# Down-projection of two token blocks by seven half-size products, with its weight and activation sums on GpSimd

## The chip, the cores and the metric

The kernel runs on one core of a Trainium2 chip. The metric is the time of one execution on the device, in microseconds. It is to be as short as possible.

## What is computed

One layer of a streaming encoder works on 2,048 prompt tokens and 128 sample tokens (8 requests of 16) of width 1,024: 17 tiles of 128 tokens. A combined projection feeds chunked attention and an mLSTM; their outputs are normalised, projected and added to the residual (the "mixers" below). Then comes a gated feed-forward part, which the change is about. In the reference:

```python
def conv_ffn(h, buf, w_up, w_conv, b_conv, w_down):
    S = h.shape[1]
    u = h @ w_up                                  # 1024 -> 2 x 2816
    ext = jnp.concatenate([buf.astype(u.dtype), u], axis=1)
    y = b_conv
    for j in range(CONV_W):                       # causal, width 3
        y = y + ext[:, j:j + S] * w_conv[j]
    gate, up = jnp.split(y, 2, axis=-1)
    out = (jax.nn.gelu(gate, approximate=True) * up) @ w_down   # 2816 -> 1024
    return out, ext[:, S:]
```

Everything is float32.

## The kernel before

**Precision.** TensorE gets its float32 operands split into a rounded high part (a cast on ScalarE, L1265) and the rest (a subtraction on VectorE, L1266). `mm3` (L93) makes one product out of three matmuls: high x high, high x low, low x high.

**Order of the work.** Python loops write out the whole program; a list scheduler then orders each engine's instructions by a simulated time line. In the mixers, projections in 14 weight groups for each half of the tokens are interleaved with steps of attention, mLSTM and normalisation. Row-wide loads there use the tile `xr`, of which there are two buffers.

**The feed-forward part** takes the tiles in three blocks: tiles 0 to 5, 6 to 11, and 12 to 15 with the sample tile. For each block:

- *Up stage* (the loop at L1478). 22 slices f of 128 features, each for gate and up. A slice is already computed as seven half-size products in Winograd's form (`product`, L1411): 7 x 4 x 3 = 84 matmuls of 384 columns. The sums of the up weights are made by VectorE in block 0 and kept in DRAM (`load_quads`, L1270 and L1282); later blocks read them. VectorE joins the products out of PSUM (L1419, L1491, L1493, L1508), does two of the convolution's three taps (L1439, L1440) and multiplies gate by up (L1514) into a tile `g` of 128 x 768. GpSimd copies the convolution's two history columns (`conv`, L1428). The tile `g` is stored to DRAM (`gd`, L1519).
- *Down stage* (the loop at L1525). For each half of the 1,024 output columns, the 22 slices of `g` are read back (`fetch`, L1454), split (`split_g`, L1465) and multiplied by weights (`load_down`, L1311) for 6 tiles at a time, in 6 PSUM accumulators. `evacuate` (L1334) copies an accumulator out on VectorE and sums its squares on ScalarE; the halves go to DRAM. Meanwhile the next block's input is normalised, transposed and summed (`h2_units`, L1057), and the previous block's outputs are finished (`later`, L1369: one operation on VectorE, an addition on GpSimd, L1377, and a store from GpSimd's queue).

**Buffers.** Loads of 512 columns use 11 "quads" (L1048), loads and results of up to 1,024 columns 4 "rows" (L1051). Nearly all loads and stores are issued in order by SyncE (SP).

Of the kernel before, what the change touches and what calls it, by code (L numbers as in the profile page):

```python
# [10 lines left out]
F32 = mybir.dt.float32  # L11
# [6 lines left out]
P = 128  # L18
# [19 lines left out]
FBLOCKS = [[0, 1, 2, 3, 4, 5], [6, 7, 8, 9, 10, 11], [12, 13, 14, 15, SAMPLE]]  # L38
HALF = [384, 384, 320]
PAIRS = [[(((b[j], 0), (b[j + 3], 0)), j * P, P, f"{b[j]}") for j in range(3)] for b in FBLOCKS[:2]]  # L40
PAIRS += [[(((12, 0), (15, 0)), 0, P, "12"), (((13, 0), (SAMPLE, 0)), P, P, "13"), (((14, 0), (14, 64)), 2 * P, 64, "14")]]


@with_exitstack
def hymba_step(ctx: ExitStack, tc: tile.TileContext, I: dict, O: dict):
# [17 lines left out]
    def dt_(shape, name):  # L63
        return dram.tile(shape, F32, tag=name, name=name)
# [48 lines left out]
    gd = [[dt_([P, 768], f"gd{b}_{f}") for f in range(NF)] for b in range(len(FBLOCKS))]  # L113
    wsd = [dt_([P, 2048], f"wsd{f}") for f in range(NF)]
    lated = [dt_([P, 4, 384], f"lated{i}") for i in range(4)]
    x2d = [dt_([P, D], f"x2d{t}") for t in range(17)]
# [928 lines left out]
        pipes[:] = [Pipe(h2_units(0, lead=6)), Pipe(iter([]))]  # L1045

    def quad(name):
        return ffn.p3.tile([P, 512], F32, tag="q", name=name, bufs=11)  # L1048

    def row(name):  # L1050
        return ffn.p3.tile([P, D], F32, tag="yq", name=name, bufs=4)  # L1051

    def new_B(i, b):
        pool = ffn.p3 if i < EARLY_B else ffn.p4
# [90 lines left out]
    def late_B():  # L1145

        for i in (P5, P2, P4, P3):
# [3 lines left out]
            nc.scalar.copy(hi, lo.bitcast(F32))  # L1151
            nc.vector.tensor_tensor(lo, lo.bitcast(F32), hi, op=ALU.subtract)

    GROUPS = ["va0", "qk0", "qk1", "va1", "qk2", "qk3", "qb0", "vo0", "qb1", "vo1", "qb2", "vo2", "qb3", "vo3"]
    SRC = {g: i for i, g in enumerate(["va0", "qk0", "qk1", "va1", "qk2", "qk3",
                                       "qb0", "vo0", "qb1", "vo1", "qb2", "vo2", "qb3", "vo3"])}
# [36 lines left out]
    chunks = []  # L1193
    norms = norm_steps(0)
    next(norms)
    pend = load_group(0)
    for _ in pend[2]:
        pass
# [2 lines left out]
    for n_, (half, gi) in enumerate(seq):  # L1201
        wh, wl, _ = pend
        split = iter([])
        if n_ + 1 < len(seq):
            pend = load_group(seq[n_ + 1][1])
            split = pend[2]
        g = GROUPS[gi]
        i = int(g[2])
        nm = f"{g}_{half}"
        if g[:2] == "va":  # L1210
            it = group_rows(wh, wl, half, chunks, vd[i], nm, 264 if gi == 0 else 256,
                            [O["v_prompt"][i], O["v_sample"][i].unsqueeze(1)])
        elif g[:2] == "qk":
            it = group_T(wh, wl, half, chunks, [qTd[i], kTd[i]], [-(DA ** -0.5), None], nm,
                         [None, [O["k_prompt"][i], O["k_sample"][i]]])
        elif g[:2] == "qb":
            it = group_T(wh, wl, half, chunks, [[t_[:, c, :] for t_ in qkbd[i]] for c in range(2)],
                         [None, DH ** -0.5], nm)
        else:
            it = group_rows(wh, wl, half, chunks, vobd[i], nm)  # L1220
        if half == 0 and gi == 13:
            chunks = []
            norms = norm_steps(1)
        if n_ == len(seq) - 1:
            out = project([0, 1, 2, 3, 4, 5, 6, 7, SAMPLE, 8, 9, 10, 11, 12, 13, 14, 15])
            split = w_out_steps()
            next(split)
            next(out)
        for u, (pe, dve) in enumerate(it):
            ahead = []  # L1230
            if n_ < len(seq) - 1 or u >= 6:
                ahead.append(next(split, (0.0, 0.0)))
            if n_ == len(seq) - 1 and u == 12:
                ahead.append(next(out))
            if (half == 0 and gi == 13 and u >= 6 and u % 2 == 0) or (gi == 0 and u % 2 == 0):
                ahead.append(next(norms, (0.0, 0.0)))
            pump(pe + sum(a[0] for a in ahead), dve + sum(a[1] for a in ahead))
        for _ in split:
            pass
        if gi == 0:  # L1240
            if half == 0:
                nc.sync.dma_start(bgate, I["b_gate"].broadcast_to([P, 8]))
                nc.sync.dma_start(gatt, I["g_att"])
                heads.append(build_bias)
                mems.append(lambda: prep(prep_sample()))
            mems.append(lambda half=half: prep(prep_prompt(half)))
        if g[:2] == "qk":
            attention(i, half)
            if half == 0 and i == 3:
                heads.insert(len(heads) % 4, lambda: attention_sample(0, EARLY))  # L1250
            if half == 1 and i == 0:
                heads.insert(len(heads) % 4, lambda: attention_sample(EARLY, DB))
        if g[:2] == "vo":
            mems.append(lambda i=i, half=half: mlstm(i, half))
            if half == 0:
                mems.append(lambda i=i: mlstm_sample(i))
# [37 lines left out]
            out.append(r)  # L1294
        return out

    def load_up(b, f, g, quads=None):
        n = 2 * f + g
# [12 lines left out]
    def load_down(dh, c):  # L1311
        n = 4 if c < 5 else 2
        src = I["w_down"][dh, 2 * c:2 * c + n // 2].rearrange("a p n -> p a n")
        h_ = wpool.tile([P, 2112], F32R, tag="wh", name=f"wdh{dh}_{c}", bufs=2)
        l_ = wpool.tile([P, 2112], F32R, tag="wl", name=f"wdl{dh}_{c}", bufs=2)
        for a in range(n // 2):
            for e in range(2):
                cc = slice(a * 1024 + e * 512, a * 1024 + e * 512 + 512)
                raw = quad(f"wdr{dh}_{c}_{a}_{e}")
                nc.sync.dma_start(raw, src[:, a, e * 512:e * 512 + 512])  # L1320
                split(h_[:, cc], l_[:, cc], raw)
        return h_, l_

    pair = [None]

# [77 lines left out]
    for b, tiles in enumerate(FBLOCKS):  # L1403
# [41 lines left out]
        def ahead_of(i):  # L1445
            if i < 2 * NF:
                pend.append(load_up(b, i // 2, i % 2))
            elif i == 2 * NF:
                pend.append(load_down(0, 0))

        g, parts = {}, {}
        n2 = nt * P // 2
# [1 line left out]
        def fetch(dh, k, early=False):  # L1454
            if dh > 1 or k >= NF:
                return
            if early:
                g[dh, k] = [quad(f"gr{b}_{dh}_{k}_{i}")[:, :n2] for i in range(2)]
                for i, r in enumerate(g[dh, k]):
                    nc.sync.dma_start(r, gd[b][k][:, i * n2:(i + 1) * n2])  # L1460
            else:
                g[dh, k] = row(f"gr{b}_{dh}_{k}")
                nc.sync.dma_start(g[dh, k][:, :2 * n2], gd[b][k][:, :2 * n2])
# [11 lines left out]
        def w3_tile(name):  # L1475
            return p4.tile([P, 1056], F32R, tag="w3", name=name, bufs=4)

        for f in range(NF):  # L1478
            w = pend.pop(0)
            ahead_of(2 * f + 2)  # L1480
            if f == NF - 2:
                fetch(0, 0, True)
                fetch(0, 1, True)
# [11 lines left out]
            uu = u_tile(f"uu{nm}")  # L1495
            second(uu, x3, c)
            w = pend.pop(0)
            ahead_of(2 * f + 3)
            if f == NF - 1:
                split_g(0, 0, w3_tile)  # L1500
                split_g(0, 1, w3_tile)
                for k in range(2, 5):
                    fetch(0, k, True)
# [15 lines left out]
            nc.sync.dma_start(gd[b][f][:, :nt * P], gt[:, :nt * P])  # L1519
# [4 lines left out]
        res = {}  # L1524
        for dh in range(2):  # L1525
            mms = [ps_mm(f"dnm{b}_{dh}_{i}") for i in range(2)]
            bigs = [ps_big(f"dn{b}_{dh}_{i}") for i in range(2)]
# [77 lines left out]
def lay_inputs(inp):  # L1605
# [15 lines left out]
    w_up = np.stack([w_up[:, :, 0, 0], w_up[:, :, 0, 1], w_up[:, :, 1, 1], w_up[:, :, 1, 0]], 2)  # L1621
    wc = np.concatenate([inp["w_conv"][0], inp["b_conv"]], 0)
    out = {
        "x_prompt": inp["x_prompt"][0],
# [11 lines left out]
        "w_down": inp["w_down"][0].reshape(NF // 2, 2, P, 2, 512).transpose(3, 0, 2, 1, 4).reshape(2, NF // 2, P, 1024),  # L1636
# [58 lines left out]
```

## Time and profile before

| | |
|---|---|
| runs, median (lowest to highest) | 2794.89 us (2793.72 to 2796.46) |
| profiled execution, first to last instruction | 2784.7 us |
| mixers up to the first up-projection | about 1313 us |
| up stage, block 0 / 1 | 328 / 318 us |
| down stage, block 0 / 1 | 195 / 194 us |
| up and down stage of the last block, to the end | 435 us |
| granted TensorE clock, mean | 0.998 |

The page gives the profiled execution's span alone; the median of the runs is 10.2 us longer, which is what lies outside the first and last instruction. In the profile PE is TensorE's matmuls, PEld its weight loads (which overlap the matmuls), DVE VectorE, ACT ScalarE, POOL GpSimd, SP SyncE. A line such as L1266 is that line of the kernel before. Stages follow each other; their ends are those of the first and last matmul of their kind.

### The profile page before, as it was taken

The numbers are of one execution on the slowest core, as the hardware profiler recorded it, in microseconds if no ns is written. First come the engines' busy times: TensorE is split into PE (matmuls) and PEld (weight loads), VectorE is DVE, ScalarE is ACT, GpSimd is POOL, SyncE is SP. The second block draws the span as 40 slices with busy tenths as digits, with TensorE's granted clock in tenths as the row PEclk, the third lists the DMA queues.
The fourth block names the chain that finished last, engine by engine and source line by source line (L and its number), as shares of the span: only waits on it lengthen the run. The fifth ranks groups of instructions, "written<-read, shape, count | busy, mean of one in ns | idle before, by whom it ended". The sixth has DMA issues, their size and how long they took to land.

```text
span 2784.7 us, 47088 instructions
## 1 busy us (share of the span) xinstructions
PE 2723.8 (98%) x16587; PEld 2548.3 (92%) x16587; DVE 1876.3 (67%) x3447; ACT 1409.1 (51%) x2836; POOL 437.4 (16%) x895
## 2 busy tenths in 40 slices
PE   8999999999999999999999999999999999999998
PEld 7899999998899998888999988899999878999887
DVE  5344455656556668666999986457877864888855
ACT  4355555644356666544454555345455543555543
POOL 1000010212000003244111110011111310222220
PEclk9999999999999999999999999999999999999999
DMA  5544355557555555356655455644544774555585
GB/s 185 155 119 136 103 174 162 164 157 217 162 173 148 144 179 171 107 176 227 187 172 167 167 176 174 219 142 153 160 152 141 276 263 152 172 179 180 192 309 190
DMA packets 311883, 486.05 MB, mean 175 GB/s; under 512 B 55426, under 2 KB 150622, under 8 KB 311518
## 3 DMA queue, kind: packets, MB, share of 16 engines
q1 hardware_dynamic: 271134, 442.92, 50.1%
q10 hardware_dynamic: 38592, 33.83, 3.6%
q0 software_dynamic: 1920, 6.29, 0.6%
q8 instruction: 130, 2.13, 0.3%
q14 instruction: 107, 0.88, 0.1%
HBM read 359.36 MB, written 126.70 MB: 175 GB/s over the span
## 4 chain that ended last, share of the span: by engine, by line
PE 55%; DVE 2%; DMA 1%; issue 1%; ACT 1%; POOL 1%; SPq 0%; DVEq 0%; POOLq 0%; ACTq 0%
PE uec L95 6%; PE uec L96 6%; PE uec L97 6%; PE dn L97 4%; PE dn L96 4%; PE dn L95 4%; PE ua L97 3%; PE ua L95 3%; PE ua L96 3%; PE dnm L97 2%; PE dnm L95 2%; PE dnm L96 2%; PE wo L97 2%; PE wo L95 2%; PE wo L96 2%; PE ub L96 1%
## 5 line engine op out<-in xcount | busy, mean ns | idle before, releaser
L95 PE MATMUL uec<-B,wuh 128*128 128x384 f32 (+1 forms) x720 | 234.9, 328 | 2.2 <-DVE uu L1419 1.1
L96 PE MATMUL uec<-B,wuh 128*128 128x384 f32 (+1 forms) x720 | 235.1, 327 | 0.0
L97 PE MATMUL uec<-B,wul 128*128 128x384 f32 (+1 forms) x720 | 233.9, 327 | 0.0
L1266 DVE TENSOR_TENSOR gl<-gr,gh 128x768 fp32r<-128x768 f32 (+3 forms) x141 | 120.4, 863 | 145.8 <-ACT gh L1265 144.5
L1265 ACT CAST gh<-gr 128x768 fp32r<-128x768 f32 (+3 forms) x141 | 102.0, 735 | 200.1 <-PE dn L96 183.2
L1265 ACT CAST wuh<-wu 128x512 fp32r<-128x512 f32 x255 | 141.7, 617 | 112.1 <-PE uec L96 103.2
L95 PE MATMUL dn<-wdh,gh 128*128 128x512 f32 x466 | 182.4, 391 | 2.3 <-DVE ug L1419 2.3
L96 PE MATMUL dn<-wdl,gh 128*128 128x512 f32 x466 | 183.4, 394 | 0.0
L97 PE MATMUL dn<-wdh,gl 128*128 128x512 f32 x466 | 167.9, 396 | 0.0
L1266 DVE TENSOR_TENSOR wul<-wu,wuh 128x512 fp32r<-128x512 f32 x255 | 164.6, 683 | 2.8 <-DMA x2d<-mx 2.8
L393 DVE CUSTOM_DVE_ANT_0 tmp<-s,nb 128x640 f32<-128x640 f32 (+4 forms) x128 | 94.4, 737 | 96.6 <-PE s L383 94.8
L95 PE MATMUL vo<-wi_h,hT 128*128 128x256 f32 x544 | 155.1, 285 | 0.6 <-DVE mt L199 0.6
L97 PE MATMUL vo<-wi_h,hT 128*128 128x256 f32 x544 | 155.6, 286 | 0.0
L96 PE MATMUL vo<-wi_l,hT 128*128 128x256 f32 x544 | 154.8, 285 | 0.0
L95 PEld LDWEIGHTS uec<-B,wuh 128*128 128x128 f32 x720 | 135.0, 188 | 4.2 <-DVE uu L1419 1.6
L95 PE MATMUL qk<-hT,wi_h 128*128 128x384 f32 (+1 forms) x384 | 128.7, 335 | 7.4 <-ACT qk_st L224 6.6
L96 PEld LDWEIGHTS uec<-B,wuh 128*128 128x128 f32 x720 | 135.2, 188 | 0.2
L97 PEld LDWEIGHTS uec<-B,wul 128*128 128x128 f32 x720 | 135.1, 188 | 0.0
L406 DVE TENSOR_TENSOR ptl<-pt,pth 128x640 fp32r<-128x640 f32 (+4 forms) x128 | 93.6, 737 | 57.1 <-ACT pth L405 56.0
L394 ACT ACTIVATE tmp<-tmp,mn 128x640 f32<-128x640 f32 (+4 forms) x128 | 97.6, 762 | 64.6 <-DVE mn L393 61.9
L96 PE MATMUL qb<-hT,wi_h 128*128 128x384 f32 (+1 forms) x384 | 127.8, 333 | 0.0
L96 PE MATMUL qk<-hT,wi_h 128*128 128x384 f32 (+1 forms) x384 | 127.6, 332 | 0.0
(412 smaller groups left out, 8873.0 us busy)
## 6 DMA issues: line engine op xcount, KB each, us to landing
wu<-in_w_up SPq DMA_DIRECT2D x220, 256.0 KB, 4.1
wu<-wsd SPq DMA_DIRECT2D x176, 256.0 KB, 4.2
wdr<-in_w_down SPq DMA_DIRECT2D x132, 256.0 KB, 5.6
gr<-gd SPq DMA_DIRECT2D x78, 384.0 KB, 3.6
wi_raw<-in_w_in SPq DMA_DIRECT2D x52, 512.0 KB, 4.0
wsd<-ws SPq DMA_DIRECT2D x88, 256.0 KB, 2.8
gd<-g SPq DMA_DIRECT2D x44, 384.0 KB, 3.5
kraw<-kTd SPq DMA_DIRECT2D x112, 128.0 KB, 3.2
```

Of the source, the lines that this page charges most:

```text
L95: nc.tensor.matmul(out, ah, bh, start=start, stop=False, skip_group_check=onto)
L96: nc.tensor.matmul(out, ah, bl, start=False, stop=False, skip_group_check=onto)
L97: nc.tensor.matmul(out, al, bh, start=False, stop=stop, skip_group_check=onto)
L393: nc.vector.tensor_tensor_reduce(o_, s_, b_, 1.0, 3e38, ALU.add, ALU.min, accum_out=mn)
L394: nc.scalar.activation(tmp[:, :n], tmp[:, :n], AF.Exp, bias=mn, scale=-1.0, accum_out=rsum[:, i % 4, hh:hh + 1])
L406: nc.vector.tensor_tensor(s.ptl[:, sl, qc], ptv, s.pth[:, sl, qc], op=ALU.subtract)
L1265: nc.scalar.copy(h, r)
L1266: nc.vector.tensor_tensor(l, r, h, op=ALU.subtract)
```

## The change

The down stage of blocks 0 and 1 takes seven products as well. With the 22 slices of `g` halved into k = 0 to 10 and 11 to 21, and the tiles into two halves of three, the activations form a 2x2 block A, and w_down forms a 2x2 block B (11 slices x 512 columns each). The seven products are A11 B11, A12 B21, S2 T2, S4 B22, S3 T3, S1 T1 and A22 T4, with S1 = A21 + A22, S2 = S1 - A11, S3 = A11 - A21, S4 = A12 - S2 and T1 = B12 - B11, T3 = B22 - B12, T2 = B22 - T1, T4 = B21 - T2 up to sign. Each is 3 tiles x 11 slices.

- `fold_down` makes T1 to T4 once, during the first half of the mixers: 22 pieces of 512 KB are read into `xr` tiles, GpSimd does four subtractions of 128x256 on each, and SP stores them to DRAM (`wtd`).
- In the up stages of blocks 0 and 1 the slices come in pairs (`FORDER`: 0, 11, 1, 12, ...). `store_a` replaces the single store of `g`: after the second slice of a pair GpSimd does four operations of 128x384 in place, and SP stores seven pieces (A11, A12, A22, S1 to S4).
- In the down stage two sets of three accumulators alternate. Three of the products are added onto a set in PSUM; `leave` copies a set out on ScalarE after products 0, 2, 4 and 6 and adds it on VectorE to a kept copy after products 1, 3 and 5. `close` sums squares and stores.
- There are 12 quads for 11 and 6 rows for 4. The scratch for descriptors of DMAs that GpSimd issues is set to 4,096 bytes.
- Block 2 keeps its down stage; only the layout of w_down in DRAM and the order of its up slices are new.

The core of the diff:

```diff
+FORDER = [f for k in range(NK) for f in (k, k + NK)]
...
+    def fold_down():
+        for k in range(NK):
+            for c in range(2):
+                cols = slice(c * 256, (c + 1) * 256)
+                t = rows_tile("xr", [P, D], f"fold{k}_{c}").rearrange("p (a n) -> p a n", a=4)
+                nc.sync.dma_start(t, I["w_down"][k].rearrange("p (a n) -> p a n", a=4)[:, :, cols])
...
+                b11, b12, b22, b21 = [t[:, i] for i in range(4)]
+                nc.gpsimd.tensor_tensor(b11, b12, b11, op=ALU.subtract)
+                nc.gpsimd.tensor_tensor(b12, b22, b12, op=ALU.subtract)
+                nc.gpsimd.tensor_tensor(b22, b22, b11, op=ALU.subtract)
+                nc.gpsimd.tensor_tensor(b21, b21, b22, op=ALU.subtract)
...
+                nc.sync.dma_start(wtd[k].rearrange("p (a n) -> p a n", a=4)[:, :, cols], t)
...
+            if half == 0 and 1 <= gi <= 12:
+                next(folds, None)
...
+    SEQUENCE = [("A11", B11, 0, False), ("A12", B21, 1, False), ("S2", T2, 0, True), ("S4", B22, 1, False),
+                ("S3", T3, 0, True), ("S1", T1, 1, False), ("A22", T4, 0, True)]
...
+        def store_a(f, gt):
+            put = lambda what, k, src: nc.sync.dma_start(ad[b, what][:, k, :], src)
+            first, second = gt[:, 0:384], gt[:, 384:768]
+            if f < NK:
+                put("A11", f, first)
+                held[f] = gt
+                return
...
+            nc.gpsimd.tensor_tensor(a11, a11, a21, op=ALU.subtract)
+            nc.gpsimd.tensor_tensor(a21, a21, a22, op=ALU.add)
+            nc.gpsimd.tensor_tensor(a22, a22, a11, op=ALU.subtract)
+            nc.gpsimd.tensor_tensor(a12, a12, a22, op=ALU.subtract)
+            for what, src in (("S3", a11), ("S1", a21), ("S2", a22), ("S4", a12)):
+                put(what, k, src)
...
+            def leave(p):
+                acc = sets[SEQUENCE[p][2]]
+                if p in (0, 2, 4, 6):
+                    kept[p] = trio(f"x{p}_")
+                for j in range(3):
+                    if p in (0, 2, 4):
+                        nc.scalar.copy(kept[p][j], acc[j])
+                    elif p == 1:
+                        nc.vector.tensor_tensor(kept[0][j], kept[0][j], acc[j], op=ALU.add)
+                        close(j, 0, kept[0][j])
...
+            for p, (_, _, set_, onto) in enumerate(SEQUENCE):
+                for c in range(3):
+                    wh, wl = pend
...
+                    for k in range(4 * c, min(4 * c + 4, NK)):
...
+                        for j in range(3):
+                            tt = slice(k % 2 * 384 + j * P, k % 2 * 384 + (j + 1) * P)
+                            mm3(sets[set_][j], ah[:, tt], al[:, tt], wh[:, wk], wl[:, wk],
+                                start=not onto and k == 0, stop=k == NK - 1, onto=onto)
```

More of the change, by code (lines that the diff above doesn't have):

```diff
@@ L1448, in ahead_of @@
             elif i == 2 * NF:
-                pend.append(load_down(0, 0))
+                pend.append(load_down(0, 0) if last else load_product(b, 0, 0))
         g, parts = {}, {}
@@ L1476, in w3_tile, with fetch_a @@
             return p4.tile([P, 1056], F32R, tag="w3", name=name, bufs=4)
-        for f in range(NF):
-            w = pend.pop(0)
[L1480 to L1483, printed above, removed]
+        def fetch_a(i):
+            if i >= 6 * len(SEQUENCE):
+                return
+            p, c = divmod(i, 6)
+            src = ad[b, SEQUENCE[p][0]]
+            ks = slice(2 * c, min(2 * c + 2, NK))
+            n_ = (ks.stop - ks.start) * 384
+            if i < 2:
+                g[i] = [quad(f"ar{b}_{i}_{x}")[:, :384] for x in range(2)]
+                for x, r in enumerate(g[i]):
+                    nc.sync.dma_start(r, src[:, 2 * c + x, :])
+            else:
+                g[i] = row(f"ar{b}_{i}")[:, :n_]
+                nc.sync.dma_start(g[i], src[:, ks, :].rearrange("p k n -> p (k n)"))
@@ new lines, in split_a @@
+        def split_a(i):
+            if i >= 6 * len(SEQUENCE):
+                return
+            r = g.pop(i)
+            n_ = 768 if isinstance(r, list) else r.shape[1]
+            h_, l_ = w3_tile(f"ah{b}_{i}")[:, :n_], w3_tile(f"al{b}_{i}")[:, :n_]
+            if isinstance(r, list):
+                for x in range(2):
+                    split(h_[:, x * 384:(x + 1) * 384], l_[:, x * 384:(x + 1) * 384], r[x])
+            else:
+                split(h_, l_, r)
+            parts[i] = h_, l_
@@ new lines, in hymba_step @@
+        held = {}
+        def store_a(f, gt):
[4 more added lines that the diff above has]
+                held[f] = gt
+                return
+            k = f - NK
+            put("A12", k, first)
+            put("A22", k, second)
+            gt1 = held.pop(k)
+            a11, a21, a12, a22 = gt1[:, 0:384], gt1[:, 384:768], first, second
+            nc.gpsimd.tensor_tensor(a11, a11, a21, op=ALU.subtract)
[4 more added lines that the diff above has]
+                put(what, k, src)
@@ L1484, in hymba_step @@
+        for fi, f in enumerate(FORDER):
+            w = pend.pop(0)
+            ahead_of(2 * fi + 2)
+            if fi == NF - 2:
+                for i in range(2):
+                    if last:
+                        fetch(0, i, True)
+                    else:
+                        fetch_a(i)
             nm = f"{b}_{f}"
@@ L1497, in hymba_step @@
             w = pend.pop(0)
[L1498 to L1503, printed above, removed]
+            ahead_of(2 * fi + 3)
+            if fi == NF - 1:
+                if last:
+                    split_g(0, 0, w3_tile)
+                    split_g(0, 1, w3_tile)
+                    for k in range(2, 5):
+                        fetch(0, k, True)
+                else:
+                    split_a(0)
+                    split_a(1)
             ug = u_tile(f"ug{nm}")
```

119 lines of the change are left out of this document (98 added, 21 removed).

## The prediction

> **What bounds the kernel now.** I read the engine shares first, then stages, then waits.
>
> ```profile
> span 2784.7 us, 47088 instructions
> ...
> PE 2723.8 (98%) x16587; PEld 2548.3 (92%) x16587; DVE 1876.3 (67%) x3447; ACT 1409.1 (51%) x2836; POOL 437.4 (16%) x895
> ```
>
> TensorE is busy 98% of the span. The share is an average, so I cut the span where the stages change: most of the mixers' first half (70 to 700 us), then up-projection and down-projection of block 0, then of block 1. The columns are length, busy time (instructions) of PE, weight loads, VectorE, ScalarE and GpSimd, granted clock, DMA share, GB/s.
>
> ```profile
> 70.00:700.00 630.00, 614.62 (x4366) 598.10 (x4364) 325.29 (x822) 312.36 (x765) 60.99 (x181) 1.00 0.51 154
> ...
> 1313.40:1641.80 328.40, 321.86 (x1826) 318.24 (x1825) 302.95 (x459) 168.51 (x268) 61.92 (x88) 0.99 0.54 178
> 1641.80:1836.40 194.60, 193.37 (x865) 157.78 (x866) 109.87 (x151) 94.19 (x157) 6.52 (x21) 1.00 0.55 181
> 1836.40:2154.80 318.40, 318.01 (x1825) 317.69 (x1823) 246.44 (x367) 163.36 (x272) 42.99 (x96) 1.00 0.48 154
> 2154.80:2349.20 194.40, 193.64 (x865) 157.04 (x866) 125.10 (x165) 91.41 (x156) 36.99 (x46) 1.00 0.68 229
> ```
>
> PE fills both down stages to 99%; its weight loads, which overlap it, take 81%, and of the other engines none is above 64%: matmuls taken out of these stages come off the time. But the up stage of block 0 is tight on a second engine: VectorE is busy 302.95 of 328.40 us, 92%. That row decides how much of the gain survives, because the change puts new work on GpSimd in that stage.
>
> **The gain: 99 matmuls in each of two stages.** Before, a block is 6 tiles x 2 halves x 22 slices x 3 = 792 matmuls of 512 columns; after, 7 products x 3 tiles x 11 slices x 3 = 693. The compiled programs agree: 2,244 down matmuls before, 2,046 after. The listed duration of a matmul overlaps the next, so I take the spacing from two starts of the same instruction in block 0, six rounds of 18 matmuls apart:
>
> ```profile
> 1803.21 0.39 PE L95 MATMUL dnm<-wdh,gh 128*128 128x512 f32 x1
> ...
> 1828.09 0.39 PE L95 MATMUL dnm<-wdh,gh 128*128 128x512 f32 x1
> ```
>
> 24.88 us / 108 = 230.4 ns. The shape of a matmul stays (128x128 stationary, 512 moving), so 198 x 0.2304 = **45.6 us** less. (The Trainium skill, "TensorE: Matmul & The Clock Gate", section "Back-to-back issue gap", gives two spacings for 512 columns, about 216 ns isolated and about 131 ns sustained; by them the gain would be 42.8 or 25.9 us. This trace shows 230.4 ns.)
>
> **Does a down stage stay on PE?** What feeds it grows. Weight splits go from 44 to 77 of 512 columns, activation splits from 44 of 768 to 77 of 384 columns (38.5 in units of 768).
>
> ```profile
> L1266 DVE TENSOR_TENSOR gl<-gr,gh 128x768 fp32r<-128x768 f32 (+3 forms) x141 | 120.4, 863 | 145.8 <-ACT gh L1265 144.5
> L1265 ACT CAST gh<-gr 128x768 fp32r<-128x768 f32 (+3 forms) x141 | 102.0, 735 | 200.1 <-PE dn L96 183.2
> L1265 ACT CAST wuh<-wu 128x512 fp32r<-128x512 f32 x255 | 141.7, 617 | 112.1 <-PE uec L96 103.2
> ...
> L1266 DVE TENSOR_TENSOR wul<-wu,wuh 128x512 fp32r<-128x512 f32 x255 | 164.6, 683 | 2.8 <-DMA x2d<-mx 2.8
> ```
>
> VectorE: +33 x 0.683 - 5.5 x 0.863 = +17.8 us; its 12 evacuation copies become 12 adds of the same width. So 128 and 143 us of about 172: 74% and 83%. ScalarE: +33 x 0.617 - 5.5 x 0.735 + 12 new copies x 0.617 = +23.7 us, 118 of 172. Loads: 33 x 262 KB more weights, 2.2 MB less activations, +6.5 MB; 44.5 + 6.5 MB in 172 us is 297 GB/s in the second stage. Higher rates already pass without costing PE anything:
>
> ```profile
> 2200.00:2215.00 15.00, 15.00 (x72) 12.29 (x71) 12.96 (x17) 10.16 (x17) 6.27 (x7) 1.00 0.98 359
> 2650.00:2660.00 10.00, 10.00 (x45) 8.10 (x44) 8.93 (x11) 4.63 (x7) 5.01 (x6) 1.00 1.04 402
> ```
>
> The two sets of accumulators alternate, so a set is emptied behind the other's 99 matmuls (22.8 us), except that sums of two products keep row buffers longer and shorten the prefetch. PE idles 1.2 and 0.8 us in these stages now; bounds 0 and 4 us more each; I take 2 each, **+4**. If the cover went (a split late by one), each product's start would show an idle gap.
>
> **What the GpSimd work costs.** Per block 44 subtractions or additions of 128x384, and 88 of 128x256 in the mixers. No row has these sizes; two others bracket them (min/median/max ns):
>
> ```profile
> L1377 POOL TENSOR_TENSOR f<-f,x x24: 1278/1560/2545, 2178.6 to 2678.6; 128x512 f32<-128x512 f32 x24
> ...
> L1027 POOL TENSOR_TENSOR mx<-mx x17: 2372/2397/2795, 1069.3 to 1319.8; 128x1024 f32<-128x1024 f32 x17
> ```
>
> The line through the two minima has (2372 - 1278) / 512 = 2.14 ns per column and 0.18 us fixed: an estimate of 1.00 us for 384 columns, 0.73 for 256. On GpSimd itself 44 us fit a stage in which it is busy 62 of 328. But the maxima are twice the minima, and the time line of down stage 1 says why:
>
> ```profile
> 2185.50 1.94 POOL L1377 TENSOR_TENSOR f<-f,x 128x512 f32<-128x512 f32 x1 [3.52 <-DVE f L1376]
> ...
> 2186.33 1.92 DVE L1266 TENSOR_TENSOR gl<-gr,gh 128x768 fp32r<-128x768 f32 x1
> ...
> 2216.22 0.95 DVE L1266 TENSOR_TENSOR gl<-gr,gh 128x768 fp32r<-128x768 f32 x1
> 2217.09 0.68 DVE L1125 TENSOR_TENSOR t<-h2T_pt,b 128x512 f32<-128x512 f32 x1
> 2217.69 1.18 DVE L1266 TENSOR_TENSOR wdl<-wdr,wdh 128x512 fp32r<-128x512 f32 x1
> ...
> 2216.39 1.93 POOL L1377 TENSOR_TENSOR f<-f,x 128x512 f32<-128x512 f32 x1 [2.82 <-DVE f L1376]
> ```
>
> The VectorE split of 768 columns takes 0.95 us alone and 1.92 us beside a GpSimd add; the add takes 1.94 instead of 1.28. They take turns. A VectorE operation that reads PSUM (h2T_pt) is not held: 0.68 us beside the second add; the split behind it waits only for the rest (1.18 for 0.68). So an add of 1.28 us costs VectorE 0.97 us in the first case (0.76 of its length), 0.50 in the second (0.39). In an up stage the first is the common case, since splits, weight differences, convolution and the product read SBUF twice and only the 5 sums of a slice read PSUM. I take 0.7 of the length, between 0 and all of it: 0.7 us for each addition of 384 columns.
>
> (The Trainium skill, "SBUF — State Buffer", section "SBUF: two separate sides", calls the port pair shared by the two engines an exclusive lock, held for the whole instruction, against VectorE operations with two SBUF inputs. This speaks against the change, and the rows agree. By it, every addition costs VectorE its full length: 303 + 44 = 347 us in up stage 0, 18.6 more than the stage has.)
>
> *Up stage 0.* 44 x 0.7 = 31 us more for VectorE, which has 328.4 - 303.0 = 25.4 us idle. Part of that idle time is usable, part is not (a group of this stage with the idle time before it, and the longest wait of PE in this stage):
>
> ```profile
> L1282 DVE TENSOR_TENSOR ws<-wu,wu 128x512 f32<-128x512 f32 x42 | 28.8, 686 | 12.4 <-DMA wu<-in_w_up 12.4
> ```
>
> ```profile
> PE ua L97 <- DVE wul L1266: 3.0, 2, 1.6
> ```
>
> 12.4 us are waits for weight loads, which a later VectorE doesn't remove, since the loads wait for buffers that it frees. The other 13.0 are waits for PE and others, and vanish when VectorE is behind. PE already waits for VectorE here (3.0 us on two splits). Ends: 31 - 25.4 = 5.6 and 31; I take 31 - 13 = **+18**. GpSimd runs in order: behind its additions stand the copies of the convolution's two history columns, and behind these VectorE's convolution. In the changed order those copies stand most of a slice (328.4 / 22 = 14.9 us) ahead of their use, so I add nothing; if GpSimd fell behind by that much, each slice's convolution would start late. SP's queue gets seven stores per pair of slices for two, and the last two wait for GpSimd with the next weights queued behind; part of the +18.
>
> *Up stage 1.* No weight differences there: 246.4 + 31 = 277 of 318 us, 87%, less than stage 0 carries today. Ends 0 and 31; nearest to stage 0 of today, whose PE idles some 6 us: **+2**.
>
> *Mixers.* 88 x 0.73 x 0.7 = 45 us of VectorE in a stretch where it is busy 325 of 630. The 22 weight pieces are read and written once, 23 MB; over some 250 us that is 92 GB/s on top of 154, below the 359 above. Against it: the additions and their stores stand in order on GpSimd and SP among the heads' loads, and early PE stalls depend on such latencies:
>
> ```profile
> PE hT_pt L67 <- DVE xr L219: 9.9, 3, 8.2
> PE qk L95 <- ACT qk_st L224: 6.6, 2, 3.3
> ```
>
> The second is an evacuation held until an earlier store has landed. Ends: -4 (the order is planned anew) and +20 (each of these waits about doubles); I take **+5**. The smaller scratch for GpSimd's own DMAs has no row; it issues 12 such transfers in each of two stages of over 140 us, so even one at a time they fit: taken as 0.
>
> **Sum.** 2784.7 - 45.6 + 4 + 18 + 2 + 5 = 2768.1 us of span. The median of the runs, 2794.89, lies 10.2 above this span; the same is kept: **2778 us**, 0.6% faster.
>
> **Rivals.**
> *All hidden.* GpSimd finds VectorE's gaps and PSUM reads: up stages +6 and 0, mixers 0, down +2: 2794.9 - 45.6 + 8 = 2757 us or less. Against: 92% busy.
> *The turns fall on the path in both up stages (slower).* If none of VectorE's idle time can be used, because its order and its loads shift with each delay, 31 us come on top in each: -45.6 + 62 + 4 + 5 = +25, 2820 us. It decides at (45.6 + 5.6 - 4 - 5) / 88 = 0.48 us per addition reaching PE; the forecast has 20 / 88 = 0.23. For it: stage 0 is nearly VectorE's already. Against: stage 1 has 72 us to spare.
> *The mixers lose it.* Head loads late behind the folding: +20 there with the rest as summed: 2793, no change.
> *The products are not fewer*: excluded by the count.
>
> **How the numbers follow.** A change of 0.2% (5.6 us) is about what a measurement tells here: faster is under 2789.3, slower over 2800.5. The forecast with costs of 10 to 40 us: 0.62. All hidden: 0.10. Mixers or part of the turns eat the rest, within 0.2%: 0.12. Turns on the path, slower: 0.16. So faster 0.72, same 0.12, slower 0.16. The range leaves about 0.1 out at each end: 2753 (costs of 4) to 2807 (costs of 58).
>
> **What would show it.** Down stages of about 173 us with PE at 98 to 99% prove the gain; longer ones with splits as PE's releaser refute it. Up stage 0 at about 346 us with VectorE 95% busy and stretched splits beside GpSimd additions prove the price; 330 us says the gaps took them. Up stage 1 near 320 us. First mixer half to within 5 us of today; a gap at head loads there would show the third rival. If the span is over 2790, the turns or the mixers are at fault, and the stage lengths say which.

## The result: slower by 1.7%

| | before | after |
|---|---|---|
| median (lowest to highest) | 2795.68 us (2793.72 to 2798.91) | 2843.13 us (2839.86 to 2845.99) |
| ratio, 95% interval | | 1.017 (1.0155 to 1.0186) |
| first up matmul | 1313.5 us | 1357.3 us |
| up stage 0, first to last matmul | 327.8 us | 353.4 us |
| down stage 0, last up matmul to next | 195.2 us | 189.9 us |
| up stage 1 | 318.0 us | 317.7 us |
| down stage 1 | 194.7 us | 187.3 us |
| from there to the end | 435.6 us | 438.0 us |
| span | 2784.7 us | 2843.6 us |

The differences of the rows, +43.8, +25.6, -5.3, -0.3, -7.4 and +2.4, are the 58.9 us between the spans. (The scheduler puts 24 up matmuls among the first down matmuls; they count to the down stage.) The fewer products brought 13 of their 45.6 us; two stages that the products don't touch lost 69. One correction belongs here: the profiled execution of before was a short one. A second profile of the same kernel had a span of 2792.9 us, and the whole difference lay in the mixers (first up matmul at 1321.7 us). The kernels changed after this one that have no fold in the mixers (below) show both values as well, 1321.2 and 1313.7 us. So some 8 of the mixers' 43.8 us are what one execution differs from the next, and about 35 are the change.

### The profile page after: what moved, and what is told of

Its sections match the earlier page's. It is cut to its first block, busy times and chain, and to the rows that moved or that the text cites. A ratio compares the mean times of both kernels' runs of the same rounds, so it can differ in the third digit from the quotient of the medians.

```text
span 2843.6 us, 47569 instructions
## 1 busy us (share of the span) xinstructions
PE 2707.8 (95%) x16389; PEld 2526.5 (89%) x16389; DVE 1942.6 (68%) x3503; ACT 1442.3 (51%) x2916; POOL 628.5 (22%) x1071
## 5 line engine op out<-in xcount | busy, mean ns | idle before, releaser
L1295 DVE TENSOR_TENSOR wdl<-wdr,wdh 128x512 fp32r<-128x512 f32 x198 | 130.2, 703 | 28.1 <-ACT wdh L1294 25.7
L99 PE MATMUL dn<-wdh,ah 128*128 128x512 f32 x308 | 123.3, 400 | 22.1 <-ACT ah L1294 21.1
L1294 ACT CAST wdh<-wdr 128x512 fp32r<-128x512 f32 x198 | 111.7, 618 | 46.8 <-DMA wdr<-in_w_down 18.7
L101 PE MATMUL qk<-hT,wi_l 128*128 128x384 f32 (+1 forms) x384 | 128.7, 335 | 0.0
L101 PE MATMUL dn<-wdh,al 128*128 128x512 f32 x308 | 124.5, 404 | 2.8 <-DVE al L1295 2.7
```

Source lines behind the costliest of these rows:

```text
L99: nc.tensor.matmul(out, ah, bh, start=start, stop=False, skip_group_check=onto)
L101: nc.tensor.matmul(out, al, bh, start=False, stop=stop, skip_group_check=onto)
L1294: nc.scalar.copy(h, r)
L1295: nc.vector.tensor_tensor(l, r, h, op=ALU.subtract)
```

## The profile after

The page opens so (busy time and share):

```profile
span 2843.6 us, 47569 instructions
...
PE 2707.8 (95%) x16389; PEld 2526.5 (89%) x16389; DVE 1942.6 (68%) x3503; ACT 1442.3 (51%) x2916; POOL 628.5 (22%) x1071
```

PE is busy 16 us less and the span is 59 us longer: PE now waits. The stages from up stage 0 to the end show where (columns as in the prediction's windows):

```profile
1357.20:1710.70 353.50, 330.48 (x1825) 320.10 (x1824) 325.91 (x457) 167.08 (x267) 113.57 (x126) 0.99 0.56 184
1710.70:1900.60 189.90, 173.76 (x767) 141.31 (x768) 128.07 (x183) 111.55 (x199) 26.34 (x34) 0.96 0.66 217
1900.60:2218.30 317.70, 317.70 (x1823) 317.39 (x1821) 252.68 (x364) 163.88 (x270) 88.33 (x130) 1.00 0.58 178
2218.30:2405.60 187.30, 174.75 (x768) 140.34 (x768) 139.56 (x194) 108.90 (x195) 48.35 (x56) 0.97 0.77 267
```

Both down stages hold about 174 us of matmuls (the prediction has 173), in stages of 190 and 187 us: 16 and 12.6 us of idle PE that were not expected. Up stage 0 has VectorE 92% busy and PE idle for 23 us; the largest group of its waits there is for a sum that VectorE makes (the same group took 0.3 us before):

```profile
PE uec L99 <- DVE x L1584: 13.2, 9, 3.3
```

In up stage 1, with the same sums, PE is never idle.

**The gap in the down stages** is one wait in each (us in total, times, longest; then SyncE's time line, its longest wait between 1700 and 1745 us, and TensorE's time line, all in the first stage):

```profile
PE dn L99 <- ACT ah L1294: 21.1, 2, 11.0
```

```profile
1719.14 0.32 SPq L1074 DMA_DIRECT2D x2r<-x2d  x1
...
1720.28 1.97 SPq L1349 DMA_DIRECT2D wdr<-in_w_down  x4
1732.19 0.33 SPq L1074 DMA_DIRECT2D x2r<-x2d  x1
1732.55 0.91 SPq L1530 DMA_DIRECT2D ar<-ad_A  x2
```

```profile
SPq L1074 <- DVE y L1479: 11.8, 2, 9.8
```

```profile
1738.30 0.80 PE L99 MATMUL dn<-wdh,ah 128*128 128x512 f32 x1 [11.04 <-ACT ah L1294]
```

SyncE stands from 1722 to 1732 us at the next block's second row (`x2r`), which waits for a row buffer that VectorE still uses for a `y` of the up stage. Behind it in order stand the third and fourth piece of A11. TensorE has work for two pieces, 4 slices x 9 matmuls x 0.2304 = 8.3 us; before, five slices of 18 matmuls were fetched ahead, 20.7 us. The named releaser is a split on ScalarE; the cause is two steps further back, in SyncE's queue.

**The mixers.** Counted by when the same matmul in order starts, after is 35 us behind the first profile of before (31 behind the second) at 210 us of the span, and little is lost later. The next rows are the first 600 us of the second profile of before and of after:

```profile
0.00:600.00 600.00, 572.25 (x4053) 560.38 (x4054) 303.29 (x735) 293.33 (x679) 49.00 (x152) 0.99 0.49 150
```

```profile
0.00:600.00 600.00, 549.17 (x3842) 535.52 (x3843) 292.75 (x676) 280.54 (x645) 111.89 (x224) 0.97 0.60 179
```

211 matmuls fewer fit. 23 us of it are idle time of PE; the rest goes with a lower granted clock (0.97 for 0.99), which falls around the gaps, as the last section shows. The waits in front of SyncE in that stretch are new:

```profile
SPq L1177 <- POOL fold L1174: 39.1, 16, 4.8
SPq L1167 <- DMA wtd<-fold: 31.4, 16, 3.6
```

Stores of folded pieces wait for GpSimd, and loads wait for the store before them to free an `xr` buffer. The first victim is the sample tile's row. Its load is issued at 36.39 us before and at 42.35 after:

```profile
36.39 0.33 SPq L212 DMA_DIRECT2D xr<-in_x_sample  x1
```

```profile
42.35 0.38 SPq L219 DMA_DIRECT2D xr<-in_x_sample  x1
```

```profile
57.03 1.97 PE L71 MATMUL hT_pt<-ident,xr 128*128 128x128 f32 x8 [10.31 <-DVE xr L226]
```

Only half of that delay is the queue. ScalarE, which waits for this load, starts on it 4.8 us after its issue before (41.22) and 11.0 us after it here (53.35): the load was also slower to land, among transfers of the fold, in a stretch that moves 278 GB/s.

## The experiments

Theories at the start: (M) the mixers lose to the fold's place in the first 230 us; (U) up stage 0 loses to GpSimd and VectorE taking turns; (D) the down stages lose to pieces 2 and 3 of A11 behind a row load. Each has a rival in the expectations below. Stage times are read as in the table. Where no interval is given, a figure is one execution, and executions of the kernel before differ by 8 us in the mixers; beside these runs that kernel took 2789 to 2797 us, so totals of different runs are compared only roughly.

**The fold left out.** `down_rows` reads plain blocks; the call of `folds` goes.

> Leaves out the weight differences T1 to T4: the fold in the mixers doesn't run, and the down stages read plain blocks of w_down in their place (same number and size of loads, so the output is not the reference's). Theory (the fold is what the mixers lose): first up matmul back at about 1313 us as before the change instead of 1357, total about 2843 - 44 = 2800 us; all later stages as in the changed kernel within 3 us. Rival (the rise of the mixers comes from the new instruction order, the buffers or the smaller scratch, not from the fold): first up matmul stays above 1345, total above 2830.

First up matmul at 1321.2 us, total 2810.9. That equals the second profile of before (1321.7), and the total stays 11 us above the expectation mostly for the same reason. The fold is the loss of the mixers; buffers, scratch and new order cost nothing there beyond the 8 us by which executions differ.

**The fold without its subtractions** (four lines removed).

> Leaves out the 88 subtractions of the fold: its 22 pieces are loaded and stored unchanged, so the T blocks hold the plain weights. Theory A (the loads and stores in SyncE's queue, their waits and bytes cost the 44 us): first up matmul within 10 us of 1357. Theory B (the subtractions cost it, by turns with VectorE or by standing in order in GpSimd's queue ahead of the first tiles' norms): within 10 us of 1313. In between, both share it in that proportion.

1342.6 us, total 2833.1: 21 us above the run with no fold, and 5 to 15 under the full fold (1347 to 1357 in the runs that have it as it was). Both share it; by these executions loads and stores alone cost more than half. Without GpSimd, SyncE stands at the stores (L1173 here) until the piece has been read:

```profile
SPq L1173 <- DMA fold<-in_w_down: 47.2, 20, 5.6
```

**The activation sums left out** (the four GpSimd operations in `store_a`).

> Leaves out the activation sums S1 to S4 (four GpSimd operations for each pair of slices, 44 for each block): all seven stores stay, and the S blocks hold plain A values. Theory (turns of GpSimd with VectorE price the first up stage): that stage back from 353 to 330 us or less, PE's waits for the sum x2 gone, total about 2820. Rival (the seven stores in SyncE's queue delay the weight loads behind them): the stage stays above 345 us. Up stage 1 (318 us) and the down stages unchanged by either.

Up stage 0: 331.7 us, total 2817.0. The sums cost 19 to 22 us (351.1 to 353.4 with them), the rest 4 to 6 (before: 325.7 and 327.8). The rest is the seven stores in place of one for each slice: kernels below with the new slice order and buffers, but block 0 in the old form, have 325.1 to 328.4. The stage's row:

```profile
1351.20:1682.90 331.70, 322.05 (x1825) 318.56 (x1823) 302.89 (x457) 167.61 (x267) 73.26 (x87) 0.99 0.61 197
```

Against after, VectorE's busy time falls from 325.91 to 302.89 us with the same 457 instructions: 44 sums on GpSimd stretch VectorE's work by 23.0 us, 0.52 us each.

**Activation pieces fetched early.**

```diff
-            if i < 2:
+            if i < 5:
                 g[i] = [quad(f"ar{b}_{i}_{x}")[:, :384] for x in range(2)]
...
                     split_a(1)
+                    for i in range(2, 5):
+                        fetch_a(i)
...
-                            if i == 0:
-                                fetch_a(2)
-                                fetch_a(3)
                             if i >= 1:
                                 split_a(i + 1)
-                            fetch_a(i + 4)
+                                fetch_a(i + 4)
```

> The whole computation. Activation pieces 2 to 4 of the first product are fetched at the end of the up stage, into quads, ahead of the next block's rows, instead of in the down stage. Theory (the down stages lose some 10 us each to pieces 2 and 3, which stand in SyncE's queue behind a row load that waits for its buffer): the gaps of PE of 11 and 10 us 28 us into each down stage are gone, down stages about 178 us instead of 188.5 and 186, total about 2822. Rival (the gap is bandwidth or the splits' engines, and only moves): down stages stay above 185 us, total above 2838.

Total 2816.4, of which part is a shorter execution of the mixers (1349.1). The gaps of 11 and 10 us are gone:

```profile
1700.10:1875.70 175.60, 171.93 (x768) 139.88 (x768) 130.18 (x186) 111.53 (x201) 25.78 (x34) 1.00 0.70 237
2193.40:2375.90 182.50, 175.90 (x769) 140.87 (x769) 141.74 (x197) 109.36 (x199) 45.41 (x56) 0.98 0.80 276
```

Theory D holds. Stage 0 is 19.6 us shorter than before, close to the predicted 20.8; stage 1 stays 8 us short of it, with 4.0 us of waits for split weights at 276 GB/s and a clock of 0.98.

**Own buffers for the fold** (two tiles of a mixer pool in place of `xr`).

> The whole computation; the fold stays where it is but works in two buffers of its own instead of the two that the tiles' norms use. Without the fold the first up matmul came at 1321 us, with its loads and stores alone at 1343, with all of it at 1349 to 1357. Theory (SyncE's queue waits for a buffer of the norms until GpSimd has folded and the store has landed, and the tiles' rows wait with it): below 1335. Rival (what stands in order in GpSimd's queue, or the bytes, costs the time, whoever owns the buffers): above 1345.

1345.2 us, total 2833.9: on the rival's edge. By this execution, whose buffers they are matters little.

**Activation sums on VectorE** (with early pieces; `gpsimd` becomes `vector` in `store_a`).

> The whole computation, with activation pieces 2 to 4 fetched early, and the 44 activation sums of each block on VectorE instead of GpSimd. Theory (a GpSimd sum costs VectorE about what the sum would cost on VectorE itself): up stage 0 stays at 345 to 355 us (351 with the sums on GpSimd, 332 without them; 44 sums at some 0.5 us are 23 us). Rival (the price is waiting for GpSimd in order, not VectorE's time): up stage 0 below 340 us. Up stage 1 stays at 318 us by both.

Up stage 0: 342.8 us, total 2805.0; between the two. The 44 sums take VectorE 0.55 us each (one of their four lines):

```profile
L1560 DVE TENSOR_TENSOR g<-g,g 128x384 f32<-128x384 f32 x10 | 5.5, 554 | 0.1
```

44 x 0.554 = 24.4 us of work cost 11.1 us of the stage (342.8 - 331.7). On GpSimd the same sums stretch VectorE by 23.0 us, no less, and cost 19.4 to 21.7. Handing them to the other engine spared VectorE nothing, and 8 to 11 us more were lost (351.1 to 353.4 against 342.8; 351.1 is the run that has the early pieces too). Where these arise (GpSimd's own order, or stretched operations at a bad moment) the runs don't tell.

**The fold in the second half of the mixers**, with early pieces, and the same with seven products in block 1 alone (`half == 1` in the call).

> The whole computation, with activation pieces 2 to 4 fetched early, and the fold moved to the second half of the mixers (groups 1 to 12 there), as it is otherwise. Theory (the fold is dear only among the first 230 us, where the first weights, rows and norms go through the same queues): first up matmul at 1315 to 1328 us, total about 2816 - 27 = 2789 us, within 0.5% of before. Rival (its subtractions and bytes cost as much anywhere): first up matmul at 1345 or later, total about 2816 or more.

> The whole computation, with the late fold and the early pieces, and seven products in block 1 alone; block 0 keeps its plain down stage and has no activation sums. Theory (block 0 gives back in its up stage, which is VectorE's, what it gains in its down stage; block 1 keeps its gain): up stage 0 at 329 us, down stage 0 at 195, up 1 at 318, down 1 at 178 to 182, first up matmul at 1315 to 1328, total 5 to 15 us under before. Rival (the late fold costs as much as the early one): total 10 us or more above before.

Both theories failed. First up matmul at 1378.5 and 1363.7 us, later than with the early fold; totals 2839.8 (ratio 1.0179, 1.0158 to 1.0200) and 2833.5 (1.0152, 1.0131 to 1.0173). Up to about 500 us these kernels run as before; from there on, with the fold's first load at 546 us in the first of them, they lose. So theory M was wrong in naming the first 230 us: the fold as written is dear anywhere in the mixers. In the second run the other stages were about as expected (328.4, 194.9, 318.0 and 182.9 us).

**The fold's loads pinned, then paced.** In after the loads of all 22 pieces are among the first 139 transfers that SyncE issues, from 23 to 241 us, though they are written over 110 steps; pinned, they go out from 32 to 437 us. The first run only pins the loads behind what is written before them. The second also has three buffers, a piece every seventh step, and distance between load, sums and store:

```diff
-                nc.sync.dma_start(t, I["w_down"][k].rearrange("p (a n) -> p a n", a=4)[:, :, cols])
+                tc.keep_in_program_order(nc.sync.dma_start(t, I["w_down"][k].rearrange("p (a n) -> p a n", a=4)[:, :, cols]))
```

```diff
+        for s in range(7 * 2 * NK + 13):
+            i, r = divmod(s, 7)
+            if r == 0 and i < 2 * NK:
+                live[i] = pa.tile([P, D], F32, tag="fold", name=f"fold{i}", bufs=3).rearrange("p (a n) -> p a n", a=4)
+                tc.keep_in_program_order(nc.sync.dma_start(live[i], half_of(I["w_down"], i)))
+            i, r = divmod(s - 9, 7)
...
+            i, r = divmod(s - 13, 7)
+            if r == 0 and 0 <= i < 2 * NK:
+                tc.keep_in_program_order(nc.sync.dma_start(half_of(wtd, i), live.pop(i)))
```

> The whole computation, with the early pieces and the activation sums on VectorE (total 2805 so far, first up matmul at 1347). Only the loads of the fold are pinned behind what is written before them on SyncE, so that the scheduler can't draw the 22 pieces together into the first 230 us; buffers, GpSimd and places as they were. Theory (crowding: the scheduler pulls the fold ahead of what is urgent): first up matmul at 1325 to 1335, total about 2790. Rival (GpSimd waiting in order for each load is what costs, as in the late fold): still 1345 or later.

> As the run before, and the fold has three buffers of its own, a piece every seventh step over the whole first half, its sums nine steps behind the load and its store four behind the sums, loads and stores pinned. Theory (what costs is waiting in the queues of SyncE and GpSimd, not the bytes or the subtractions): first up matmul at 1313 to 1325, total 2772 to 2784, under before. Rival (turns of VectorE and GpSimd, or bytes, cost it): 1335 or later.

Pinned: 1359.2 us, total 2811.6, no better, as its rival has it; the loss only spreads to 440 us. Paced: 1336.7 us, total 2793.2 beside 2797.5 for before on that chip. The theory's 1313 to 1325 was missed, and by the letter of the expectation this is the rival's figure (1335 or later); but 22 us of the pinned run's loss are gone with the same bytes and the same subtractions. The waits of SyncE and GpSimd on the fold in the first 600 us, pinned and then paced:

```profile
SPq L1177 <- POOL fold L1174: 32.0, 14, 4.0
...
SPq L1177 <- DMA fold<-in_w_down: 23.4, 6, 6.3
...
POOL fold L1171 <- DMA fold<-in_w_down: 194.8, 21, 39.9
```

```profile
SPq L1179 <- POOL fold L1176: 4.3, 3, 2.9
...
SPq L1169 <- DMA wtd<-fold: 2.0, 2, 1.2
...
POOL fold L1173 <- DMA fold<-in_w_down: 201.7, 16, 35.1
```

GpSimd stands as long in front of the fold's loads in both. SyncE does not: all its waits on the fold are some 60 us against 9. And the paced fold moves more bytes in that stretch, at a better clock:

```profile
0.00:600.00 600.00, 564.93 (x3976) 550.38 (x3977) 311.94 (x719) 286.08 (x661) 121.11 (x236) 0.99 0.60 186
```

So neither the bytes (186 GB/s against 179 in the pinned run) nor GpSimd's waiting nor its subtractions is the main price here. What fell with it is SyncE's standing in front of a store or a load of the fold, with everybody's loads behind it. Pace, pins, distance and buffers were changed together, so this is the account that fits and not one shown by itself. The pace is hardly the point: a run below loads its fold from 35 to 416 us, as fast as the pinned one, and is 19 us behind the first profile of before at 600 us where the pinned one is 41. (Its subtractions are on VectorE, which moved the first up matmul by 3 to 4 us in the runs that follow.)

**The paced fold on VectorE**, and timed again.

> As the run before, with the fold's 88 subtractions on VectorE. If what is left of the fold's price is GpSimd's queue or the turns: first up matmul some 5 to 10 us earlier than in that run. If it is bytes or SyncE's queue: within 4 us of it.

> The kernel with the fold in every seventh step on VectorE, timed for an interval: one look gave 2792.2 beside 2797.5 for before, a ratio of 0.998. Theory: 0.996 to 1.000; first up matmul within 4 us of 1334.

1333.8 and 1333.1 us, 3 to 4 us before the fold on GpSimd, so by the expectation turns are not what is left. The two outcomes lie closer together than executions do, so that is weak evidence. Total 2792.2 in the first execution; the median of eleven is 2788.3 against 2789.9, ratio 0.9996 (0.9987 to 1.0005): no difference that can be measured.

**A faster pace: five steps to a piece, four in a kernel with block 1 alone; and block 1 alone at the pace of seven.**

> The whole computation: both blocks by seven products, early pieces, sums and fold on VectorE, three buffers, pinned, and a piece every fifth step instead of every seventh, so that the fold is over by some 400 us, before the stretch from 417 to 764 us in which the slower pace lost its last 14 us. Theory (a fold among work that PE covers costs nothing): first up matmul at 1321 to 1327, total 2780 to 2787, 0.2 to 0.5% under before. Rival (the faster pace crowds the first 230 us again): 1335 or later, total 2793 or more.

> Seven products in block 1 alone, fold and sums on VectorE, a piece every fourth step. Its mixers show the price of a still faster pace: at most 1327 us to the first up matmul if PE covers it, 1335 or more if it crowds; stages from there on as in the run with block 1 alone (up 0 at 326, down 0 at 195, up 1 at 320, down 1 at 183).

> The whole computation: seven products in block 1 alone (block 0 keeps its plain down stage), early pieces, sums on VectorE, paced fold on GpSimd. Against the run with the same fold and both blocks: up stage 0 at 329 us instead of 343, down stage 0 at 195 instead of 176, so 5 us longer in all, if a block's gain and price are as measured; the rest within 3 us.

1330.1, 1332.4 and 1334.6 us; the first two lie between the two expectations for their pace, the third is within 3 us of its own. Against the first profile of before the pace of five loses 15 us up to 417 us and 1 after, the pace of seven 3 to 8 and then 12 to 18; the end is much the same: with the two runs at seven steps above, 8 to 15 us over the second profile of before. What that rest is made of stays open. Five steps, median of eleven: 2792.6 against 2789.9, ratio 1.0013 (1.0003 to 1.0022), so the theory's 2780 to 2787 failed. By medians the pace of seven is 4.3 us ahead, although its profile has the longer mixers: the profile at five steps is the shortest of its eleven executions, the one at seven the second longest. Block 1 alone at the pace of seven gave 2802.1, 9 us more than both blocks at that pace (2793.2) where 5 were expected: up stage 0 is 15 us shorter (325.1), down stage 0 17 longer (194.9), and the other stages together are 7 longer. At the pace of four it gave 2799.6. In its own two stages, block 0 by seven products gains 2 us in these executions: it is worth little more than it costs.

**The kernel before, once more.**

> The kernel before, once more, as a control for what the mixers' length is worth from one run to the next. Without any fold the changed kernel had its first up matmul at 1321 us, before it was at 1313. If this run gives 1318 or more, those 8 us are what a profile varies by; if it gives 1313 within 2 us, they belong to the changed kernel's order of instructions in the mixers, with or without the fold.

1321.7 us, span 2792.9, 1.7 us under its own time: by the expectation, the variation of an execution, used throughout above.

**The fold in block 0's plain down stage** (block 1 alone takes seven products).

> The whole computation: seven products in block 1 alone, early pieces, sums on VectorE, and the fold in block 0's plain down stage (VectorE there is busy 110 of 195 us; loads and stores of the fold add 23 MB to 181 GB/s, about 300 GB/s in all), in its row buffers. Theory (queue space beside steady work is cheap): first up matmul as before at 1313 to 1322, up stage 0 at 326, down stage 0 at 195 to 203, down stage 1 at 183, total 2778 to 2790, under before by 0 to 0.5%. Rival (the down stage's own loads wait behind the fold's): down stage 0 at 210 or more, total above 2795.

Mixers as before (1313.7 us), up stage 0 at 325.7, and down stage 0 at 210.5 us instead of 195.2:

```profile
1639.40:1849.90 210.50, 196.55 (x866) 158.88 (x866) 143.19 (x241) 95.11 (x158) 8.83 (x22) 0.99 0.80 279
```

PE idles 14 us, where VectorE is busy 68%; its longest waits are for the next block's rows (`x2r`, 6.7 us) and for splits of `g` (5.4 us). Total 2795.0 against 2789.5, ratio 1.0024 (1.0015 to 1.0033). The stage came out at the rival's figure. No place that was tried makes the fold free.

## Why the prediction was wrong

- **Fewer matmuls, 45.6 us: right.** Matmul time in the down stages fell by 19.6 and 18.9 us in after (at a clock of 0.96 and 0.97), and by 21.4 in a stage at full clock (the early fetch, block 0), where 22.8 were forecast.
- **"I take 2 each" for the down stages: wrong.** 22.8 us of matmuls less shortened them by 5.3 and 7.4, so the term measured 17.5 and 15.4. Longer stages with a split as PE's releaser are the very sign that the text gives as a refutation. It compared engines and bytes over the whole stage, and it named a shorter prefetch and a split late by one, but priced them at 2. It did not count what is fetched ahead when the stage begins (8.3 us of work for 20.7) or what stands before the rest in SyncE's queue. With the early fetch the terms are 3.2 and 10.4.
- **Up stage 0, +18: right in mechanism, short in size**, 25.6 (27.7 against the second profile). Of its parts: VectorE's stretch was 23.0 us, not 31; of its idle time 13 were held usable, and the VectorE variant bears that out (24.4 of work, 11.1 on the path). But on GpSimd they cost 19 to 22, and the stores, put inside the 18, 4 to 6 more. The estimates for one sum held for the fastest ones: 0.72 us for 256 columns (0.73 was taken), 0.99 for 384 (1.00). The stretch per sum of 384 was 0.52 us where 0.7 was taken. (By the Trainium skill, "SBUF — State Buffer", section "SBUF: two separate sides", whichever of the two engines' operations starts first holds the port pair for its whole length. The prediction took from it that every sum costs VectorE its full length; the 23.0 us measured for 44 sums are about half of the 44 us that they take by the prediction's clean estimate, so that reading was an upper bound.)
- **Up stage 1, +2: right** (-0.3).
- **Mixers, +5 with ends -4 and +20: this step failed.** It measured 43.8, some 35 beyond the variation. Leaving out the fold gives all of it back. The ends came from two waits of TensorE that exist before, and 8.2 us of the larger one are the start of the span, before the first matmul, which no fold can double. The fold's own chain was not priced: load, four sums, store, next load through two buffers, each link a wait at the head of SyncE's in-order queue (86 us of SyncE's waits on it in the first 600 us, and 9 in the paced run, which loses 22 us less than the pinned one). The third rival named late head loads, but priced them at 20 by doubling those two waits. The 250 us over which the text spread the fold were right (23 to 248 us). What the last 8 to 15 us are, with the fold paced, stays open.
- **The 10.2 us outside the span: wrong.** An execution takes about 2 us more than its span (2845.43 for 2843.6, 2794.62 for 2792.9). The profiled execution of before was itself some 8 us shorter than the median, and the second profile puts that in the mixers. As the 10.2 were added on both sides, this did not shift the forecast difference.
- **The rival "turns on the path in both up stages"** got the sign, but not the cause: up stage 1 lost nothing. With the measured terms the prediction's own sum gives -45.6 + 32.9 (down stages) + 25.6 - 0.3 + 35 (mixers, beyond the variation) = 47.6 us, and 50 with the 2.4 of the last block; the medians differ by 47.5. This is bookkeeping on the same profiles: it shows where the time went and no cause.

## To carry to other kernels

Work put into "idle" queues is priced by what it makes the in-order queue wait for: write down, for each added DMA, the event it waits for at the head of its queue and what stands behind it. When a stage is rewritten, count how many microseconds of work are fetched before it starts, old and new. And a saving in one stage must carry the preparation it needs elsewhere: in the best kernel here (fold paced and on VectorE, early fetch) 31 us of shorter down stages paid for some 11 us of the fold, 13 to 15 in up stage 0 and some 5 in the later stages, and little was left.

## What the runs showed of the chip beyond that

The granted clock falls around TensorE's gaps. In after it is 0.74 in the 20 us that hold the gap before 57 us, and 0.92 in the next 20, in which PE is 99% busy again. The second pair of rows is finer: the clock is 0.50 to 63 us, six us after the matmuls are back, and 1.00 from there:

```profile
40.00:60.00 20.00, 8.68 (x64) 8.07 (x62) 2.92 (x5) 3.96 (x7) 7.03 (x14) 0.74 0.95 278
60.00:80.00 20.00, 19.76 (x112) 18.88 (x113) 8.42 (x38) 2.76 (x8) 7.60 (x11) 0.92 0.70 221
```

```profile
57.00:63.10 6.10, 4.97 (x18) 4.57 (x19) 1.23 (x1) 1.01 (x1) 0.00 (x0) 0.50 0.99 251
63.30:80.00 16.70, 16.56 (x103) 15.68 (x102) 7.19 (x37) 2.72 (x7) 7.60 (x11) 1.00 0.65 207
```

A gap so costs more than its length. It does not do so each time, and much of the 8 us between the two profiles of before is that. Both have a gap that ends at 83 to 84 us; the first runs on at full clock, the second does not and falls from 1.1 to 3.3 us behind in five us. Around a gap at 710 us it loses 3.5 more in the same way (0.79 against 1.00 from 704 to 720 us). The rows of the two around the first gap:

```profile
80.00:90.00 10.00, 6.97 (x39) 6.71 (x40) 3.98 (x12) 3.54 (x7) 0.00 (x0) 1.00 0.40 102
```

```profile
80.00:90.00 10.00, 6.51 (x23) 5.74 (x22) 3.06 (x9) 2.88 (x6) 0.00 (x0) 0.66 0.27 68
```

The other surprise is that 44 sums cost VectorE as much when GpSimd does them (23.0 us) as when VectorE does (24.4 us).
